# Summing the squares of twelve later norms on VectorE, and head norm pieces at half the rate

## The chip, the cores and the metric

The kernel runs on one core of one Trainium2 chip. The time is that of one execution on the device, in microseconds; several executions are taken and their median is given. One more execution is recorded by the hardware profiler, and everything called a row or a profile comes from that one.

## The reference

Two layers of a diffusion backbone run over 1024 latent tokens and 128 context tokens, 1024 channels each. What matters here is what stands at the start and the end of each half layer, and the norm of the attention heads:

```python
def rmsnorm(x, g):
    xf = x.astype(jnp.float32)
    y = xf * lax.rsqrt(jnp.mean(xf * xf, axis=-1, keepdims=True) + EPS)
    return y.astype(x.dtype) * g

def diff_head_out(o, subln_g, lam_init):
    o = rmsnorm(o, subln_g) * (1.0 - lam_init)        # per head, 128 channels

hc = modulate(rmsnorm(ctx, norm_g[i, 1]), m_ctx[3], m_ctx[4])
ctx = ctx + m_ctx[5] * sq_relu_mlp(hc, ff_w1[i], ff_w2[i])
...
y_prompt = rmsnorm(ctx, final_norm_g)
```

Layer 0 mixes its tokens by differential attention beside a state-space scan, layer 1 by a pooling mixer; each is followed by an MLP with 4096 hidden channels and a squared ReLU.

## The kernel before

The 1152 tokens lie in three blocks `b` of 384 (`BN`); block 2 holds 256 latent and 128 context tokens. Channels lie on the partitions, so `x[b]` is eight tiles (`k`) of 128 channels by 384 tokens, and a norm must add over the eight tiles and over the 128 partitions of each. The big products split each fp32 operand into a high and a low part (`blk`, `wh`/`wl`, `ph`/`pl`, all fp32r) and multiply three pairs of parts, so that TensorE's plain work comes in triples of 384-column products.

The norms that the change touches are the later ones: before the first MLP (norm 1), before the pooling mixer (norm 2), before the second MLP (norm 3) and at the end, each for three blocks, twelve in all. `norm_sums` is called with `done=False` for them. For each `k` ScalarE squares `x[b][k]` into a small tile (`r`, two of them; `ph` and `pl` for the final norms of blocks 1 and 2), and TensorE multiplies the square by a 128x32 tile of ones, on one of four column strips of the array (`tile_position`), into `nps`. So the sums of tiles `k` and `k + 4` stand on strip `k`. ScalarE copies `nps` to `s4`, and one product with `selbc`, in which only rows 0, 32, 64 and 96 hold 1/1024, adds the four strips and spreads the mean over all partitions (`npb`). `norm_root` then takes its -1/2 power in two ScalarE and four VectorE steps into `y`. The norms of the very first stage take `done=True`: their squares are made ahead, and they stay as they are.

The high and low parts of a block (`gains`: ScalarE writes `h_`, VectorE `l_`) don't need `y`, since `y` is multiplied in behind the first product of the MLP (`r<-p,y`). In a chunk of the MLP VectorE makes `r`, `s` and `pl` for every hidden tile and adds each second product to `x` (`x<-p,modc,x`); in the first MLP it also takes column sums for the modulation of layer 1 (`mj`).

The order of the work: a planner orders the instructions of each engine at build time, by its own costs, and the engines then run their queues in that order, each waiting for what an instruction needs. Only where an engine is pinned does it keep the order in which the code is written. In the attention, TensorE alone is pinned (`PINA = "T"`).

The attention loop has one step per block of 128 queries: nine per head (eight latent, one context), four heads, 36 in all and four more to drain. In a step TensorE computes the scores of block `i` (`SP`), transposes those of three steps before (`tp`), and multiplies by the values. VectorE takes the maxima (`nm`) and combines the two maps (`e`), ScalarE takes exponentials. When the last block of a head is done, `head_norm` of that head is appended to `norms`. It is a generator with nine pieces: the set-up of the root on [128, 9] numbers (`vv`), two pieces with two Newton steps each, and for each of three groups of blocks one piece in which VectorE scales `of` and one in which TensorE transposes it, ScalarE copies it to `og` and a store to `cS` is issued. The loop asks for pieces at the end of every step. The last head's run behind the loop, where nothing is pinned.

All instructions are recorded through one helper, so that their line in the profile is L86; tiles tell them apart.

Of the kernel before, what the change touches and what calls it, by code (L numbers as in the profile page):

```python
# [8 lines left out]
F32 = mybir.dt.float32  # L9
F32R = mybir.dt.float32r  # L10
I32 = mybir.dt.int32
AF = mybir.ActivationFunctionType
ALU = mybir.AluOpType
# [4 lines left out]
D = 1024  # L18
KT = 8
# [3 lines left out]
BN = 384  # L23
# [49 lines left out]
def build(nc, tc, a, o, probe=None):  # L73
    pinned = set()

    class Engine:
# [5 lines left out]
        def __getattr__(self, op):  # L82
            f = getattr(self.e, op)

            def call(*args, **kw):
                ins = f(*args, **kw)  # L86
                if self.name in pinned:
# [5 lines left out]
    V, A, T, P, S_ = (Engine(n, e) for n, e in (("V", nc.vector), ("A", nc.scalar), ("T", nc.tensor),  # L93
                                                ("P", nc.gpsimd), ("S", nc.sync)))
# [25 lines left out]
    def tt(e, out, x, y, op):  # L120
        return e.tensor_tensor(out, x, y, op=op)
# [19 lines left out]
    selbc = K([128, 128], F32, "selbc")  # L141
# [35 lines left out]
    GB = [2]  # L177
# [8 lines left out]
    psn = Pool("psn", side="left", space=PSUM)  # L186
# [69 lines left out]
    last_bc = [None]  # L256
# [2 lines left out]

    def norm_sums(xb, sq, s4, done=False):  # L260

        ps = psn([128, BN], F32, "nps", bufs=GB[0], tag="g")
        for k in range(KT):
            if not done:
                A.activation(sq(k), xb[k], AF.Square)
            g = k % 4
            T.matmul(ps[32 * g:32 * g + 32], ones32, sq(k, True), start=k < 4, stop=k >= 4, tile_position=(0, 32 * g))
        A.activation(s4, ps, AF.Copy)
        pb = psn([128, BN], F32, "npb", bufs=GB[0], tag="g")
        last_bc[0] = T.matmul(pb, selbc, s4, start=True, stop=True)  # L270
        return pb

    def norm_root(pb, y, u):

        A.activation(y, pb, AF.Ln, bias=epsc)
        A.activation(y, y, AF.Exp, scale=-0.5)
        tt(V, u, y, y, ALU.mult)
        stt(V, u, pb, epsc, u, ALU.add, ALU.mult)
        V.tensor_scalar(u, u, -0.5, 1.5, op0=ALU.mult, op1=ALU.add)
        tt(V, y, y, u, ALU.mult)  # L280
        return y

    def sq_tile(more=False):
        last = []

        def sq(k, again=False):
            if not again:
                last[:] = [hid([128, BN], F32, ("ph", "pl")[k % 2]) if more else HP([128, BN], F32, "r", bufs=2)]
            return last[0]

        return sq

    def norm_stats(xb, more=False):
        pb = norm_sums(xb, sq_tile(more), HP([128, BN], F32, "s", bufs=2))
        return norm_root(pb, HP([128, BN], F32, "y", bufs=YB[0]), HP([128, BN], F32, "s", bufs=2))

# [76 lines left out]
    def sums(b):  # L373
        return norm_sums(xs[b], lambda k, again=False: sqs[b][:, k], scratch(), True)
# [273 lines left out]
    for gi, g0 in enumerate(range(0, G, 3)):  # L648
        n = min(3, G - g0)
        for ri in range(2):  # L650
            p = pin_([128, 3, UC], F32, "pin", bufs=2)
            for j in range(n):
                g = g0 + j
# [90 lines left out]
    psn = Pool("psn", side="left", space=PSUM)  # L744
# [273 lines left out]
    def scores(i, m):  # L1018

        h, qb = work[i]  # L1020
        Q, Kd, Kl, Vv, l1 = hd[h]
        q0 = 128 * qb
        if m == 0:
            cur[i] = (AT([128, 2], F32, "nm", bufs=2), AT([128, 1], F32, "ll", bufs=2), [])
        nm, ll, ee = cur[i]
        if qb < 8:
            cuts, n, k0 = ((0, 512), (512, 1024), (1024, KEYS)), KEYS, 0
        else:
            cuts, n, k0 = ((0, TX),), TX, KEYS
        for c0, c1 in cuts:  # L1030
            T.matmul(SP[m][:, c0:c1], Q[m][:, q0:q0 + 128], Kd[m][:, k0 + c0:k0 + c1], start=True, stop=False)
            T.matmul(SP[m][:, c0:c1], Q[m][:, q0:q0 + 128], Kl[m][:, k0 + c0:k0 + c1], start=False, stop=True)

    def top(i, m):
        n = KEYS if work[i][1] < 8 else TX
        V.tensor_reduce(cur[i][0][:, m:m + 1], SP[m][:, 0:n], AX.X, ALU.max, negate=True)

    def exps(i, m):
        nm, ll, ee = cur[i]
        n = KEYS if work[i][1] < 8 else TX  # L1040
        e = AT([128, KEYS], F32, f"e{m}", bufs=4 - 2 * m)
        sum_ = ll[:, 0:1] if m else hd[work[i][0]][4][:, work[i][1]:work[i][1] + 1]
        last_set[0] = A.activation(e[:, :n], SP[m][:, 0:n], AF.Exp, bias=nm[:, m:m + 1], accum_out=sum_)
        ee.append(e[:, :n])

    def ratio(i):

        h, qb = work[i]
        ll = cur[i][1]
        cf = AT([128, 1], F32, "cf", bufs=2)  # L1050
        V.reciprocal(cf, ll)
        V.tensor_scalar(cf, cf, hd[h][4][:, qb:qb + 1], lamn, op0=ALU.mult, op1=ALU.mult)
        cur[i] = (cf, cur[i][2])

    def combine(i):
        cf, ee = cur.pop(i)
        stt(V, ee[0], ee[1], cf, ee[0], ALU.mult, ALU.add)
        st[i] = ee[0]
# [3 lines left out]
    def turn(i, k0):  # L1062

        if k0 == 0:
            wt[i] = AT([128, 10, 128], F32, "wt", bufs=2)
        n = 4 if work[i][1] < 8 else 1 - k0 // 4
        if n == 0:
            return
        pt = pT([128, 4, 128], F32, "tp", bufs=2)
        for j in range(n):  # L1070
            T.transpose(pt[:, j], st[i][:, 128 * (k0 + j):128 * (k0 + j + 1)], ident)
        A.activation(wt[i][:, k0:k0 + n], pt[:, :n], AF.Copy)

    def values(t, i):

        po = pT([128, 4, 128], F32, "tp", bufs=2)
        two = t < nw and work[t][1] < 8
        if two:
            for j in range(2):
                T.transpose(po[:, j], st[t][:, 128 * (8 + j):128 * (9 + j)], ident)  # L1080
        if i >= 0:
            h, qb = work[i]
            Vv = hd[h][3]
            nk = 10 if qb < 8 else 1
            for k in range(nk):
                T.matmul(po[:, 2], wt[i][:, k], Vv[:, k if qb < 8 else 10], start=k == 0, stop=k == nk - 1)

        def copies():
            if two:
                A.activation(wt[t][:, 8:10], po[:, 0:2], AF.Copy)  # L1090
            if i >= 0:
                if h not in ofs:
                    ofs[h] = RP([128, 9, 128], F32, "of", tag=("cos", "sin")[h % 2]), AT([128, 4, 9], F32, "vv", bufs=2)
                A.activation(ofs[h][0][:, qb], po[:, 2], AF.Copy)

        def squares():
            if i >= 0:
                of, vv = ofs[h]
                V.scalar_tensor_tensor(RP([128, 128], F32, "sq", tag="sc1"), of[:, qb], 1.0, of[:, qb], op0=ALU.mult,
                                       op1=ALU.mult, accum_out=vv[:, 3, qb:qb + 1])  # L1100

        return copies, squares
# [81 lines left out]
    loads, norms, done = None, [], None  # L1184
# [7 lines left out]
    for i, t in enumerate(turns):  # L1192
        if i == 1:
            pinned.update(PINA)
        v, tv = (tv, t) if t >= 0 else (-1, tv)
        if i < nw:
            h, qb = work[i]
            scores(i, 0)
            top(i, 0)
        if done:  # L1200
            done[0]()
        if 1 <= i <= nw:
            ratio(i - 1)
        if done:
            done[1]()
        if 0 <= t < nw:
            turn(t, 0)
        if i < nw:
            scores(i, 1)
            top(i, 1)  # L1210
        if 0 <= t < nw:
            turn(t, 4)
        if i < nw:
            exps(i, 0)
        if SO and i >= 2:
            next(side, None)
        if 1 <= i <= nw:
            combine(i - 1)
        if i < nw:
            exps(i, 1)  # L1220
        if not SO and i >= 2:
            next(side, None)
        done = values(t, v) if t >= 0 else None
        for _ in range(2):
            if norms and next(norms[0], 0) == 0:
                norms.pop(0)
        if v >= 1 and work[v - 1][1] == 8:
            norms.append(head_norm(work[v - 1][0]))
        if i < nw:
            if qb == 3 and h + 1 < HEADS:  # L1230
                loads = load_head(h + 1)
            if loads:
                next(loads, None)
# [29 lines left out]
    XP = Pool("xp", side="left")  # L1263
    BB = Pool("blkB", side="left")
    HP = Pool("hid", side="right")
    psn = Pool("ps2", side="left", space=PSUM)
    GB[0] = 2
    YB[0] = 3
# [8 lines left out]
    p2 = lambda shape: psn(shape, F32, "p2", bufs=4)  # L1277
    hid = lambda shape, dt, nm: HP(shape, dt, nm, bufs=4)
    cb = HP([128, 2, D], F32, "cb")

# [12 lines left out]
    def mod_vec(layer, t):  # L1293
# [4 lines left out]
        for r in range(2):  # L1298
            V.scalar_tensor_tensor(HP([128, D], F32, "mj"), raw, 1.0, cb[:, r], op0=ALU.mult, op1=ALU.mult,
                                   accum_out=modc[layer][:, t, r:r + 1])  # L1300
# [426 lines left out]
```

## Time and profile before

| | us |
|---|---|
| median of 3 executions | 2579.72 |
| lowest, highest | 2579.07, 2583.84 |
| profiled execution | 2578.7 |
| its span, first to last instruction | 2576.9 |
| TensorE products busy | 2449.6 (95%) |
| VectorE busy | 1748.6 (68%) |
| ScalarE busy | 883.8 (34%) |
| GpSimd busy | 259.6 (10%) |

Busy time is an average over stages with different limits. PE is TensorE's products, PEld its weight loads, DVE is VectorE, ACT ScalarE, POOL GpSimd. A product of two plain fp32 operands leaves two records, one of fp32r operands one. Products are pipelined, so the length of a record is longer than the distance to the next one; the distance between starts tells what the queue spends.

### The profile page before, as it was taken

The numbers are of one execution on the slowest core, as the hardware profiler recorded it, in microseconds if no ns is written. First come the engines' busy times: TensorE is split into PE (matmuls) and PEld (weight loads), VectorE is DVE, ScalarE is ACT, GpSimd is POOL, SyncE is SP. The second block draws the span as 40 slices with busy tenths as digits, with TensorE's granted clock in tenths as the row PEclk, the third lists the DMA queues.
The fourth block names the chain that finished last, engine by engine and source line by source line (L and its number), as shares of the span: only waits on it lengthen the run. The fifth ranks groups of instructions, "written<-read, shape, count | busy, mean of one in ns | idle before, by whom it ended". The sixth has DMA issues, their size and how long they took to land.

```text
span 2576.9 us, 36670 instructions
## 1 busy us (share of the span) xinstructions
PE 2449.6 (95%) x14262; PEld 2295.9 (89%) x14262; DVE 1748.6 (68%) x3498; ACT 883.8 (34%) x1675; POOL 259.6 (10%) x274
## 2 busy tenths in 40 slices
PE   7987897887899999999999999999999999999998
PEld 3876696787897999999999999779999999999996
DVE  7389875888687776877777655676555656555554
ACT  4453365776515222222222222562222222222114
POOL 5455512100000000000000000020000000000002
PEclk8998999999999999999999999999999999999999
DMA  6334689331263222222222110011111111011102
GB/s 241 83 107 130 190 199 235 71 92 48 78 225 116 73 82 79 84 83 81 90 80 89 50 33 25 1 50 42 50 41 42 50 33 50 33 50 42 42 9 74
DMA packets 106493, 210.89 MB, mean 82 GB/s; under 512 B 10576, under 2 KB 67664, under 8 KB 105936
## 3 DMA queue, kind: packets, MB, share of 16 engines
q1 hardware_dynamic: 104080, 203.01, 26.4%
q10 hardware_dynamic: 2240, 5.54, 0.6%
q8 instruction: 113, 1.85, 0.3%
q14 instruction: 60, 0.49, 0.1%
HBM read 176.95 MB, written 31.56 MB: 81 GB/s over the span
## 4 chain that ended last, share of the span: by engine, by line
PE 72%; DVE 7%; issue 4%; ACT 3%; DMA 3%; POOL 0%; SPq 0%; DVEq 0%; ACTq 0%; POOLq 0%
PE p L86 65%; PE nps L86 2%; PE pmm L86 2%; PE tp L86 1%; DVE nm L86 1%; ACT e L86 1%; PE SP L86 1%; DMA raw<-in_w_dram 1%; DVE e L86 1%; DMA raw<-in_mod_v_dram 1%; PE py L86 1%; DVE sc L86 1%; DVE mj L86 1%; DVE x L86 0%; DVE wl L86 0%
## 5 line engine op out<-in xcount | busy, mean ns | idle before, releaser
L86 PE MATMUL p<-blk,wh 128*128 128x384 f32 (+1 forms) x3072 | 794.9, 339 | 0.3 <-DVE r L86 0.3
L86 DVE SCALAR_TENSOR_TENSOR x<-p,modc,x 128x384 f32<-128x384 f32 (+2 forms) x1056 | 513.2, 513 | 162.7 <-PE p L86 158.5
L86 PEld LDWEIGHTS p<-blk,wh 128*128 128x128 f32 x3072 | 559.1, 189 | 13.3 <-issue 11.9
L86 PE MATMUL p<-blk,wl 128*128 128x384 f32 (+1 forms) x1536 | 521.4, 339 | 0.0
L86 PE MATMUL p<-ph,w2h 128*128 128x384 f32 x1536 | 515.1, 335 | 1.6 <-DVE x L86 1.6
L86 PE MATMUL p<-ph,w2l 128*128 128x384 f32 x1536 | 514.3, 335 | 0.0
L86 PE MATMUL p<-pl,w2h 128*128 128x384 f32 x1536 | 513.7, 334 | 0.0
L86 ACT ACTIVATE r<-r,cf 128x384 f32<-128x384 f32 (+2 forms) x256 | 129.9, 531 | 684.9 <-DVE r L86 684.8
L86 PEld LDWEIGHTS p<-blk,wl 128*128 128x128 f32 x1536 | 288.8, 188 | 6.5 <-issue 6.3
L86 PEld LDWEIGHTS p<-ph,w2h 128*128 128x128 f32 x1536 | 288.3, 188 | 6.9 <-DVE x L86 3.5
L86 PEld LDWEIGHTS p<-ph,w2l 128*128 128x128 f32 x1536 | 288.3, 188 | 2.6 <-issue 2.5
L86 PEld LDWEIGHTS p<-pl,w2h 128*128 128x128 f32 x1536 | 288.3, 188 | 0.8 <-issue 0.6
L86 DVE TENSOR_TENSOR r<-p,y 128x384 f32<-128x384 f32 x192 | 106.2, 553 | 207.4 <-PE p L86 194.3
L86 ACT ACTIVATE wh<-raw 128x1024 fp32r<-128x1024 f32 x80 | 84.8, 1060 | 346.1 <-PE p L86 312.2
L86 DVE SCALAR_TENSOR_TENSOR mj<-raw,cb 128x1024 f32<-128x1024 f32 x128 | 156.0, 1219 | 14.0 <-DMA raw<-in_mod_v_dram 12.9
L86 ACT ACTIVATE w2h<-raw 128x1024 fp32r<-128x1024 f32 x74 | 77.3, 1057 | 223.3 <-PE p L86 159.0
L86 PE MATMUL pmm<-lo,wh 128*128 128x384 f32 (+1 forms) x384 | 137.8, 359 | 7.3 <-DVE lo L86 7.1
L86 PE MATMUL pmm<-hi,wh 128*128 128x384 f32 (+1 forms) x384 | 141.3, 369 | 0.8 <-ACT wh L86 0.8
L86 PE MATMUL pmm<-hi,wl 128*128 128x384 f32 (+1 forms) x384 | 137.0, 357 | 1.2 <-DVE wl L86 1.2
L86 DVE TENSOR_TENSOR s<-r 128x384 f32<-128x384 f32 x192 | 106.4, 554 | 39.3 <-ACT r L86 39.1
L86 POOL TENSOR_TENSOR pl<-pl,mx 128x256 f32<-128x256 f32 x18 | 14.9, 827 | 1070.0 <-ACT pl L86 1070.0
L86 DVE TENSOR_TENSOR wl<-raw,wh 128x1024 fp32r<-128x1024 f32 x76 | 98.8, 1300 | 23.1 <-ACT wh L86 22.7
(281 smaller groups left out, 3348.7 us busy)
## 6 DMA issues: line engine op xcount, KB each, us to landing
raw<-in_w_dram SPq DMA_DIRECT2D x128, 512.0 KB, 3.6
raw<-in_mod_v_dram SPq DMA_DIRECT2D x64, 512.0 KB, 3.6
raw<-in_mod_w_dram SPq DMA_DIRECT2D x25, 512.0 KB, 4.9
raw<-in_w_in_dram SPq DMA_DIRECT2D x16, 512.0 KB, 4.8
Kd<-kS SPq DMA_DIRECT2D x32, 176.0 KB, 5.1
qS<-zz SPq DMA_DIRECT2D x12, 384.0 KB, 2.7
Q<-qS SPq DMA_DIRECT2D x32, 144.0 KB, 5.2
x<-in_x_dram SPq DMA_DIRECT2D x3, 1536.0 KB, 7.7
```

The lines of the kernel that those rows point to most:

```text
L86: ins = f(*args, **kw)
```

## The change

`norm_sums` with `done=False` no longer multiplies the squares by ones. The square of the first tile goes straight to `s4`, and VectorE adds the squares of the other seven tiles to it, one by one. A single product with `selbc` sums over the partitions and spreads. For that `selbc` is filled with 1/1024 in all rows after the attention. `nps` and its copy are gone for these twelve norms. In the attention loop one piece of the head norms is asked for per step, not two.

```diff
--- before.py
+++ after.py
@@ -259,10 +259,16 @@
 
     def norm_sums(xb, sq, s4, done=False):
 
+        if not done:
+            A.activation(s4, xb[0], AF.Square)
+            for k in range(1, KT):
+                A.activation(sq(k), xb[k], AF.Square)
+                tt(V, s4, s4, sq(k, True), ALU.add)
+            pb = psn([128, BN], F32, "npb", bufs=GB[0], tag="g")
+            last_bc[0] = T.matmul(pb, selbc, s4, start=True, stop=True)
+            return pb
         ps = psn([128, BN], F32, "nps", bufs=GB[0], tag="g")
         for k in range(KT):
-            if not done:
-                A.activation(sq(k), xb[k], AF.Square)
             g = k % 4
             T.matmul(ps[32 * g:32 * g + 32], ones32, sq(k, True), start=k < 4, stop=k >= 4, tile_position=(0, 32 * g))
         A.activation(s4, ps, AF.Copy)
@@ -1221,9 +1227,8 @@
         if not SO and i >= 2:
             next(side, None)
         done = values(t, v) if t >= 0 else None
-        for _ in range(2):
-            if norms and next(norms[0], 0) == 0:
-                norms.pop(0)
+        if norms and next(norms[0], 0) == 0:
+            norms.pop(0)
         if v >= 1 and work[v - 1][1] == 8:
             norms.append(head_norm(work[v - 1][0]))
         if i < nw:
@@ -1263,6 +1268,7 @@
     XP = Pool("xp", side="left")
     BB = Pool("blkB", side="left")
     HP = Pool("hid", side="right")
+    V.memset(selbc, 1.0 / D)
     psn = Pool("ps2", side="left", space=PSUM)
     GB[0] = 2
     YB[0] = 3
```

## Rows read from the trace of the kernel before

**Rows 1.** The page's chain that ended last, by line: share of the span.

```profile
PE p L86 65%; PE nps L86 2%; PE pmm L86 2%; PE tp L86 1%; DVE nm L86 1%; ACT e L86 1%; PE SP L86 1%; DMA raw<-in_w_dram 1%; DVE e L86 1%; DMA raw<-in_mod_v_dram 1%; PE py L86 1%; DVE sc L86 1%; DVE mj L86 1%; DVE x L86 0%; DVE wl L86 0%
```

**Rows 2.** Windows: length, then busy us of PE, PEld, DVE, ACT, POOL; clock, DMA.

```profile
795.00:840.00 45.00, 44.42 (x200) 28.40 (x199) 31.27 (x67) 29.72 (x64) 0.00 (x0) 1.00 0.22 71
840.00:1606.00 766.00, 764.43 (x4363) 763.09 (x4362) 538.24 (x1032) 171.29 (x276) 0.00 (x0) 1.00 0.23 71
1606.70:1655.00 48.30, 48.30 (x246) 37.10 (x244) 34.13 (x76) 30.61 (x64) 0.00 (x0) 1.00 0.00 1
1655.00:1684.00 29.00, 27.20 (x200) 22.75 (x200) 15.08 (x45) 12.83 (x32) 7.71 (x11) 1.00 0.01 2
1684.00:1756.00 72.00, 69.62 (x405) 50.31 (x404) 50.62 (x142) 45.21 (x99) 16.03 (x20) 1.00 0.16 51
2514.00:2534.00 20.00, 20.00 (x99) 14.72 (x98) 6.42 (x12) 8.73 (x18) 0.00 (x0) 1.00 0.00 1
2546.00:2562.30 16.30, 16.30 (x84) 10.89 (x84) 8.25 (x22) 11.76 (x26) 3.21 (x4) 1.00 0.12 41
```

**Rows 3.** Groups of instructions, whole span: busy us, mean ns, idle before.

```profile
L86 DVE TENSOR_TENSOR s<-r 128x384 f32<-128x384 f32 x192 | 106.4, 554 | 39.3 <-ACT r L86 39.1
...
L86 PE MATMUL nps<-r,ones 128*32 128x384 f32 x160 | 51.8, 498 | 0.8 <-ACT r L86 0.8
...
L86 ACT ACTIVATE r<-x 128x384 f32<-128x384 f32 x80 | 39.4, 518 | 42.5 <-PE nps L86 35.7 <-DVE x L86 6.8
```

**Rows 4.** Timeline of PE in the first norm: start us, us, instruction.

```profile
797.88 0.34 PE L86 MATMUL p<-blk,w2l 128*128 128x384 f32 x1
...
798.41 0.33 PE L86 MATMUL p<-blk,w2l 128*128 128x384 f32 x1
798.68 0.84 PE L86 MATMUL nps<-r,ones 128*32 128x384 f32 x4
799.45 0.62 PE L86 MATMUL p<-blk,w2h 128*128 128x384 f32 x2
799.90 0.33 PE L86 MATMUL p<-blk,w2l 128*128 128x384 f32 x1
...
800.34 0.83 PE L86 MATMUL nps<-r,ones 128*32 128x384 f32 x2
801.10 0.44 PE L86 MATMUL p<-blk,w2h 128*128 128x384 f32 x1
```

**Rows 5.** Timeline of DVE, POOL and ACT at the end.

```profile
2560.55 2.03 DVE L86 SCALAR_TENSOR_TENSOR x<-p,modc,x 128x256 f32<-128x256 f32 x6
...
2566.78 1.14 DVE L86 TENSOR_TENSOR s<-y 128x384 f32<-128x384 f32 x1 [4.20 <-ACT y L86]
...
2560.77 8.01 POOL L86 TENSOR_TENSOR x<-x,y 128x384 f32<-128x384 f32 x8 [13.09 <-ACT ph L86]
...
2564.12 0.49 ACT L86 ACTIVATE s<-nps 128x384 f32<-128x384 f32 x1 [0.92 <-PE nps L86]
2565.62 0.58 ACT L86 ACTIVATE y<-npb,epsc 128x384 f32<-128x384 f32 x1 [1.00 <-PE npb L86]
```

**Rows 6.** Waits of PE in the attention (total, times, longest), and three in its timeline.

```profile
PE tp L86 <- DVE of L86: 21.3, 4, 8.1
...
536.32 0.88 PE L86 MATMUL tp<-ident,of 128*128 128x128 f32 x3 [5.19 <-DVE of L86]
...
597.32 0.88 PE L86 MATMUL tp<-ident,of 128*128 128x128 f32 x3 [8.13 <-DVE of L86]
...
659.77 0.88 PE L86 MATMUL tp<-ident,of 128*128 128x128 f32 x3 [7.64 <-DVE of L86]
```

**Rows 7.** Windows right behind the three waits, columns as in Rows 2.

```profile
536.30:545.00 8.70, 8.68 (x49) 8.53 (x50) 2.76 (x11) 3.70 (x10) 0.00 (x0) 0.66 0.33 105
597.30:604.00 6.70, 6.68 (x44) 6.56 (x45) 3.50 (x12) 3.50 (x10) 0.00 (x0) 0.78 0.42 137
659.70:665.00 5.30, 5.23 (x26) 5.26 (x27) 2.40 (x8) 2.68 (x7) 0.00 (x0) 0.50 0.59 229
```

## The prediction

> **What bounds the kernel now.** I read the chain of waits first: TensorE holds nearly all of it, 65% in the plain products `p` alone, and `PE nps`, the products that sum a norm's squares, stand in it with 2%, some 50 us [rows 1]. Next the busy times by stretch, cut where the later norms lie [rows 2]: 795 to 840 us (the three norms before the first MLP), 1606.7 to 1655 and 1655 to 1684 (the three before pooling), 1684 to 1756 (the three before the second MLP), 2514 to 2534 and 2546 to 2562.3 (the final norms). The reader is to see two things. TensorE is busy through each of them (44.4 of 45, 48.3 of 48.3, 27.2 of 29, 69.6 of 72, 20 of 20, 16.3 of 16.3 us), so an instruction that leaves its queue there shortens the run unless something else is late. VectorE, which gets the new work, is busy 31.3, 34.1, 15.1, 50.6, 6.4 and 8.3 us of the same stretches: there is room, but not in all of them. The span is 2576.9 us, the profiled execution took 2578.7, and the median of the three runs is 2579.72, 1.0 above it; I sum against 2578.7 and add 1.0.
>
> **Removed: eight products per norm.** The table of groups [rows 3] gives 51.8 us of TensorE for ten of the twelve norms (160 records; each fp32 product leaves two), but a busy time doesn't say what the queue loses, so I count in the timeline [rows 4]. A plain triple `wh, wh, wl` repeats every 0.53 us (797.88 to 798.41). With one group of `nps` between, the same step takes 1.49 us (798.41 to 799.90): 0.96 us lost per group, since the queue pauses before and after it. A group of four records costs what a group of two does (798.68 to 799.45 is 0.77, 800.34 to 801.10 is 0.76). So the price goes by groups. Of such groups I count, in the stretches before the tail, 17 (three norms), 12 (two), 5, 20 (three) and 6, together 60 in ten norms; 60 x 0.95 = 57 us.
>
> A rule speaks for a smaller price: the Trainium skill, "TensorE: Matmul & The Clock Gate", Packing small matmuls, has tiles on different columns of the array run at once, four for little more than one. The row of four records agrees. By the rule alone a norm is two packs of four products, 2 x 0.77, ten norms are worth 15 us, and the time would be 42 us later, 2567. The trace differs because the squares come one at a time through two tiles, and so the products stand in five to seven groups; the measured 57 decides.
>
> The product with `selbc` stays, as do the squares. The copy to `s4` (ScalarE, 0.49 us, [rows 5]) goes; ScalarE isn't the bound in these stretches.
>
> **Added: seven additions per norm on VectorE.** The nearest row is `s<-r`, the same shape, SBUF to SBUF: 0.554 us [rows 3]; in a chain with itself a little more, 0.6. 84 of them are 47 to 50 us of VectorE. They are free where it idles and cost where it would then be the later engine. By stretch, with TensorE's time shortened by the groups:
> - 795 to 840: 45 - 16.2 = 28.8 us for TensorE; VectorE 31.3 + 21 x 0.554 = 42.9. 14 us too much. Part of it can wait: the column sums `mj` aren't needed at once, and the MLP behind leaves VectorE 766 - 538 = 228 us idle [rows 2]. What can't wait are the splits `blk`, the roots and `r, s, pl` of the first block. I take a loss of 5 (bounds 0 and 14).
> - 1606.7 to 1655: 48.3 - 11.4 = 36.9 against 34.1 + 7.8 = 41.9. 5 over; it holds back results that TensorE's accumulators wait for. Loss 4.
> - 1655 to 1684: 24.2 against 19.0. No loss.
> - 1684 to 1756: 72 - 19 = 53 against 50.6 + 11.6 = 62.2. 9 over, some of it passed on to the second MLP. Loss 6.
> - 2514 to 2534: 14.3 against 10.3. No loss.
>
> **The wait that is added.** The one product with `selbc` now waits for VectorE's last addition, and TensorE keeps its queue's order: plain products behind it wait too, and with them VectorE's next results. The trace shows no such wait. It is nothing where the planner puts the product late enough, and at most the whole chain, 0.52 + 7 x 0.6, about 5 us, where it stands right behind the squares. I take 0.2 us per norm, 2 in all, since the wait that it replaces (for the copy `s`) is mostly hidden too. The tiles of the squares are freed by VectorE now instead of TensorE, and `s4` is held from the first square on; both belong to tags of two that the MLP shares, which is in the same bounds.
>
> Ten norms: 57 - 5 - 4 - 6 - 2 = 40 us, between 15 and 57.
>
> **The tail.** VectorE writes the last parts of `x` until 2562.6, the copy `s` starts at 2564.12 and the first step of the root at 2565.62 [rows 5]. With the change TensorE gets through the last blocks about 5 us earlier, but VectorE must fit 14 additions, 7.8 us, into the 16.3 us in which it has 8.3 of work [rows 2]: it ends about when it ended before, and the copy goes (0.5). The danger is GpSimd: while it multiplies (2560.77 on), `s<-y` takes 1.14 instead of 0.55 us, so seven additions in its company cost 4 more. I take 1 us gained, bounds -4 and +5. The Trainium skill, "SBUF — State Buffer", Who interferes with whom, says that a VectorE instruction with two SBUF inputs contends with a GpSimd one that reads SBUF; the row agrees. By that rule all of the last norm's additions would be slow and the tail 4 us longer.
>
> **Head norm pieces, one per block.** TensorE runs in written order in the attention. Its largest waits there are `tp` for `DVE of`, 21.3 us in four [rows 6]: three stand before a head's first head norm transposes, 5.19, 8.13 and 7.64 us at 536, 597 and 660. The scaled `of` comes late because the twenty small steps of the root are strung between long VectorE instructions, and with two pieces a block the transposes follow the first step by two blocks only. With one a block they follow by four; a block is about 5.9 us ((597.32 - 536.32 - 8.13) / 9 between the first head norm transposes of two heads, the second stall taken off), so the small steps get some 12 us more and the stall should go. What is late next is VectorE, which was busy through the stalls. But it starves behind them, being busy only 2.76 of 8.7, 3.50 of 6.7 and 2.40 of 5.3 us, and TensorE comes out of them partly at the lower of its two clocks (granted 0.66, 0.78 and 0.50, against 1.00 in the stretches of [rows 2]) [rows 7]. 20.7 - 8.7 = 12 us of VectorE's idle time bound what the first two can give back. Behind the third TensorE is full to the end of the stage, so nearly all 7.6 us come back. Of head 2 one piece (three transposes, a copy, a store) falls behind the loop, under 1 us. I take 14, bounds 0 and 24. Memory traffic and other queues are the same: the stores `cS` move one to five blocks later and are read after the stage.
>
> **Sum.** 40 + 1 + 14 = 55; 2578.7 - 55 + 1.0 = 2524.7, say 2525 us.
>
> **Rivals.**
> - The additions cost twice what I take off. In the norm windows VectorE is 28 us over; if all of it comes back as TensorE waits instead of 15, and each `npb` waits 1.5 us, the norms give 57 - 28 - 15 = 14, and with the heads 28: 2552. For it: three stretches in which VectorE becomes the longer engine. Against: `mj` and the weight splits ahead of need can move.
> - The head norms give nothing, because VectorE sets the pace of the attention and the small steps are as many as before: 2539. Against: the idle time behind the stalls.
> - Nothing is lost: 57 + 5 + 24 = 86, so 2494. For it: before, the norms' latency was no shorter (eight squares at 0.52 us, each waiting for its product).
> - Slower than before: TensorE reaches the product with `selbc` early and stands there for the chain at every norm, while the additions queue on VectorE behind splits and `mj`. Its place is `npb`, its price the wait; it wins from the point where a norm's wait and what VectorE holds back exceed (57 + 14) / 10 = 7.1 us. With a 5.3 us chain and the 28 us over, that is 8.1 a norm: 2590. Against: VectorE is idle for 13.7 us of the first stretch and 14.2 of the second, and the planner counts the additions when it places the product.
> - That the planner, with other costs, reorders the work so that nothing moves: no change.
>
> **How the numbers follow.** Forecast with its own range of 2508 to 2538: 0.60. Heads give nothing: 0.12 (it lies at that range's upper edge). Additions cost twice: 0.13. Nothing lost: 0.09. No change: 0.02. Slower: 0.04. A range of 2500 to 2553 leaves out most of the fourth, half of the third and the last two, under 0.2. 0.2%, about what a measurement here tells from no change, is 5 us: faster 0.94, same 0.02, slower 0.04.
>
> **What would show it.** No `nps` on TensorE after 100 us; plain triples at 0.53 us right up to `npb`; 84 additions `s<-s,r` (or `ph`, `pl`) of about 0.55 us; no wait of `tp` for `of` above 1 us before the last head; VectorE's idle time in 795 to 830 near zero. I am wrong if TensorE waits at `npb` by more than 2 us a norm, if `r<-p` or `x<-p` become what TensorE waits for at the start of an MLP, if the attention's length stays, or if the end from VectorE's last `x` to the first step of the root grows beyond 3 us.

## The result: half of the gain that was forecast

| | before | after |
|---|---|---|
| median, lowest to highest, us | 2579.73, 2579.07 to 2583.84 | 2552.59, 2551.55 to 2554.24 |
| profiled execution, its span | 2578.7, 2576.9 | 2552.8, 2551.0 |
| TensorE, VectorE busy | 2449.6, 1748.6 | 2399.8, 1792.0 |

The ratio is 0.9892 (95% 0.9875 to 0.9909): 27 us faster, where 55 were forecast. The time lies at the upper edge of the stated range, 2500 to 2553, and outside the forecast's own, 2508 to 2538. To see where it differs I cut both traces at the same four events: the load of the Ln/Exp table behind the attention, the first `cf` of the first MLP's second-last chunk (what norm 1 does is in by then), the first band product of pooling (`p<-mx,ph`), the first 128x386 product of the second MLP. Lengths in us:

| stretch | before | after | difference | forecast |
|---|---|---|---|---|
| start to table load (attention) | 705.1 | 688.9 | -16.2 | -14 |
| table load to `cf` (norm 1) | 830.3 | 831.0 | +0.7 | -11 |
| `cf` to pooling's first band product (most of norm 2) | 132.0 | 127.0 | -5.0 | -10 |
| to the second MLP (rest of norm 2, norm 3 blocks 0 and 1) | 67.0 | 66.0 | -1.0 | -8 |
| second MLP to the end (norm 3 block 2, final norms) | 842.5 | 838.1 | -4.4 | -13 |

The forecast's column is its own terms: groups removed less VectorE's overrun, and 1 us for the tail in the last row, without the 2 us for waits at `npb`. The groups are put where they lie in the trace before, 17, 15, 15 and 13 in the last four rows, at 0.95 us each. So the attention did a little better than forecast, and the norms with the tail gave 9.7 us instead of 41.

How far such differences can be trusted is seen where two kernels share their code behind the attention: the kernel before and the run with the new head norm pieces alone (below) agree within 0.4 us in each of the last four stretches, the changed kernel and the run with the new norms alone within 2.1 us.

The waits of TensorE say why: first those in the attention (480 to 700 us), then those from 760 us to the end, each with total, times and longest. They answer to [rows 6].

```profile
PE SP L86 <- ACT e L86: 13.8, 18, 2.2
PE tp L86 <- ACT of L86: 1.9, 1, 1.9
...
PE npb L86 <- DVE s L86: 37.4, 7, 10.3
PE p L86 <- DVE w2l L86: 4.3, 1, 4.3
PE p L86 <- DVE x L86: 3.7, 6, 0.9
```

`tp` no longer waits for VectorE's `of`: 21.3 us are gone, 1.9 for ScalarE have come, and the waits of `SP` for `e` have grown from 11.7 to 13.8 us. And `npb` waits 37.4 us for VectorE's sums; before it waited 1.2 us in all, for the copy. Here is one such place, the start of the first MLP, in the timeline: TensorE, then VectorE and ScalarE.

```profile
805.46 0.33 PE L86 MATMUL p<-blk,wl 128*128 128x386 f32 x1
810.69 1.27 PE L86 MATMUL npb<-s,selbc 128*128 128x384 f32 x2 [4.89 <-DVE s L86]
820.35 1.65 PE L86 MATMUL npb<-s,selbc 128*128 128x384 f32 x2 [8.39 <-DVE s L86]
...
822.44 0.52 PE L86 MATMUL p<-blk,wl 128*128 128x384 f32 x1
...
806.84 0.56 DVE L86 TENSOR_TENSOR s<-s,r 128x384 f32<-128x384 f32 x1
807.32 1.22 DVE L86 SCALAR_TENSOR_TENSOR mj<-raw,cb 128x1024 f32<-128x1024 f32 x1
...
808.46 0.56 DVE L86 TENSOR_TENSOR s<-s,r 128x384 f32<-128x384 f32 x1
808.93 1.22 DVE L86 SCALAR_TENSOR_TENSOR mj<-raw,cb 128x1024 f32<-128x1024 f32 x1
...
810.08 0.56 DVE L86 TENSOR_TENSOR s<-s,r 128x384 f32<-128x384 f32 x1
...
811.70 1.22 DVE L86 TENSOR_TENSOR wl<-raw,wh 128x1024 fp32r<-128x1024 f32 x1
...
817.29 1.22 DVE L86 TENSOR_TENSOR w2l<-raw,w2h 128x1024 fp32r<-128x1024 f32 x1
818.42 1.88 DVE L86 TENSOR_TENSOR s<-s,r 128x384 f32<-128x384 f32 x3
820.22 1.01 DVE L86 TENSOR_TENSOR r<-p,y 128x384 f32<-128x384 f32 x2
...
809.05 0.52 ACT L86 ACTIVATE r<-x 128x384 f32<-128x384 f32 x1 [1.09 <-DVE s L86]
```

An addition takes 0.56 us as forecast, but the next one starts 1.62 us later (806.84, 808.46, 810.08). Two things are seen in between: a column sum `mj` of 1.22 us on VectorE, and a square on ScalarE that could only start when the addition had freed one of the two `r` tiles. That square is done at 809.57, while `mj` keeps VectorE until 810.08, so here it is `mj` that sets the pace. Where nothing stands between, three additions take 1.88 us (818.42). The second and longer wait, 8.39 us, has no `mj` in it: there the root of block 1 and two weight splits of 1.22 us (`wl`, `w2l`) stand beside the additions. TensorE has computed block 0's two hidden tiles by 805.8, and the two products `npb` (blocks 1 and 2) stand next in its queue. What would empty the accumulators, `r<-p,y`, writes the same two `r` tiles and comes only at 820.22, behind the last addition.

The waits cost more than their length. These are windows of the stretch before the second MLP (columns as in [rows 2]):

```profile
1663.00:1712.93 49.93, 40.59 (x268) 37.38 (x267) 43.13 (x118) 31.77 (x70) 16.40 (x18) 0.79 0.16 52
1672.00:1674.00 2.00, 0.00 (x0) 0.00 (x0) 2.00 (x7) 2.00 (x5) 0.00 (x0) 1.00 0.00 0
1676.00:1678.00 2.00, 1.91 (x4) 0.74 (x4) 2.00 (x5) 0.57 (x2) 0.00 (x0) 0.50 0.00 0
1682.00:1684.00 2.00, 2.00 (x11) 2.00 (x11) 0.76 (x3) 0.00 (x0) 0.09 (x1) 0.50 0.00 0
1688.00:1690.00 2.00, 2.00 (x20) 2.00 (x19) 1.12 (x4) 0.00 (x0) 0.00 (x0) 1.00 1.00 397
```

TensorE stands from 1671.8 to 1675.75 for `npb`; behind that its granted clock is 0.50, the lower of its two levels (1.2 GHz), until about 1685. In 2 us it gets through 11 products at that clock and 20 at 1.00. Before, the clock was 1.00 all through ([rows 2], fourth and fifth line). VectorE is at 2.00 of 2.00 while TensorE stands, and 43.1 us busy of 49.9 in the whole window.

Not every loss shows as a wait for `npb`. In the stretch before pooling there is none; there TensorE waits the 4.3 us for `w2l`, and 3.3 us in five shorter waits, four of them for VectorE.

The end, first VectorE's last `x` and its additions, then TensorE, ScalarE and GpSimd; it answers to [rows 5].

```profile
2530.00 0.34 DVE L86 SCALAR_TENSOR_TENSOR x<-p,modc,x 128x128 f32<-128x128 f32 x1
2530.26 0.55 DVE L86 TENSOR_TENSOR s<-s,pl 128x384 f32<-128x384 f32 x1
2530.84 1.23 DVE L86 TENSOR_TENSOR s<-s,ph 128x384 f32<-128x384 f32 x1
...
2537.24 1.16 DVE L86 TENSOR_TENSOR s<-s,pl 128x384 f32<-128x384 f32 x1
...
2538.46 1.65 PE L86 MATMUL npb<-s,selbc 128*128 128x384 f32 x2 [10.29 <-DVE s L86]
...
2540.20 0.58 ACT L86 ACTIVATE y<-npb,epsc 128x384 f32<-128x384 f32 x1 [9.22 <-POOL x L86]
...
2530.22 9.99 POOL L86 TENSOR_TENSOR x<-x,y 128x384 f32<-128x384 f32 x8 [12.77 <-ACT ph L86]
```

From the last `x` (2530.34) to the first step of the root 9.9 us pass, against 3.0 before (2562.58 to 2565.62). All seven additions come behind the last `x`; VectorE did block 1's root and `x` first. Six of them take 1.16 to 1.23 us beside GpSimd's products, instead of 0.55. The Trainium skill, "SBUF — State Buffer", Who interferes with whom, says that a VectorE instruction with two SBUF inputs contends with a GpSimd one that reads SBUF. Those six rows agree.

### The profile page after: what moved, and what is told of

The parts are those of the page before. It is cut to its first block, busy times and chain, and to the rows that moved or that the text cites. A ratio compares the mean times of both kernels' runs of the same rounds, so it can differ in the third digit from the quotient of the medians.

```text
span 2551.0 us, 36404 instructions
## 1 busy us (share of the span) xinstructions
PE 2399.8 (94%) x14070; PEld 2296.1 (90%) x14070; DVE 1792.0 (70%) x3583; ACT 877.2 (34%) x1663; POOL 267.0 (10%) x274
## 4 chain that ended last, share of the span: by engine, by line
PE 64%; DVE 11%; issue 5%; ACT 4%; DMA 4%; POOL 1%; SPq 0%; POOLq 0%; DVEq 0%; ACTq 0%
PE p L86 61%; DVE mj L86 2%; DVE blk L86 1%; DMA raw<-in_w_dram 1%; DVE sc L86 1%; DMA raw<-in_mod_v_dram 1%; PE SP L86 1%; DVE nm L86 1%; ACT e L86 1%; PE tp L86 1%; DVE x L86 1%; DVE s L86 1%; ACT blk L86 1%; DVE zz L86 1%; DVE w2l L86 1%
## 5 line engine op out<-in xcount | busy, mean ns | idle before, releaser
L86 DVE SCALAR_TENSOR_TENSOR mj<-raw,cb 128x1024 f32<-128x1024 f32 x128 | 156.1, 1220 | 13.6 <-DMA raw<-in_mod_v_dram 12.6
```

## Experiments

Every ratio is against the kernel before on the same chip; the changed kernel stands at 0.9892.

**The two parts alone.**

```diff
 # heads only: kernel before, with
-        for _ in range(2):
-            if norms and next(norms[0], 0) == 0:
-                norms.pop(0)
+        if norms and next(norms[0], 0) == 0:
+            norms.pop(0)
 # norms only: changed kernel, with these lines as before
```

> The head norm pieces one per block alone, the later norms as before. The trace of the changed kernel reaches the table load at the attention's end 16.2 us earlier (688.88 against 705.10), so if the two parts don't touch each other: 2579.7 - 16.2 = 2563.5 us. Rival: the gain of the attention is there only because what follows it is shorter too (loads that the norms' buffers free earlier); then 2570 or more.

Measured: 2560.07, ratio 0.9927 (0.9910 to 0.9943), 18.0 us.

> The later norms changed, the head norm pieces two per block as before. If the parts are independent, 2552.6 + 16.2 = 2568.8 us, a gain of 11 where 41 was forecast. Rival: the norms lose because they come earlier against the loads behind the attention; then alone they gain more, 2560 or less.

Measured: 2569.01, ratio 0.9964 (0.9951 to 0.9977), 9.1 us. 18.0 + 9.1 is the 27.1 of both; with intervals of 3 to 4 us to either side the sum shows that the parts are independent within that, not to the last digit. The norms are where the forecast's gain is missing.

**Wait or work?** Two theories: TensorE loses by standing at `npb` (and by the clock behind it), or VectorE is simply the longer engine and `npb` is where it shows.

```diff
 # e3: the same additions, but npb doesn't wait for them (not in the final norms)
-                tt(V, s4, s4, sq(k, True), ALU.add)
+                d = s4 if key[0] == 4 else sq(k, True)
+                tt(V, d, s4, sq(k, True), ALU.add)
...
 # e4: TensorE has something to do while it would stand
+            for _ in range(5 if key in ((1, 1), (1, 2), (3, 0), (3, 1), (3, 2)) else 0):
+                T.matmul(pb, selbc, xb[7], start=True, stop=True)
             last_bc[0] = T.matmul(pb, selbc, s4, start=True, stop=True)
...
```

> As the changed kernel, but in the nine middle norms (before the first MLP, before pooling, before the second MLP) each of the seven additions adds the first square to its own square tile, so VectorE does the same number of additions of the same shape, and the product with selbc takes the first square alone. Seven eighths of the sum are left out there; the final norms are untouched. Wait theory (what the change loses is TensorE standing at npb behind a drawn-out chain of additions, and the lower clock that follows): the 27.2 us of waits at npb in these norms go, and some 14 us of half speed behind them (20 us of the stretch before the second MLP and 8 of the first MLP at 0.50, worth half): about 2511 us. VectorE theory (VectorE is the longer engine there, and npb only the place where it shows): TensorE then waits for r<-p,y, blk or x instead, and at most 8 us come back: 2545 to 2553.

Measured: 2538.62, ratio 0.9843 (0.9828 to 0.9858), between the two. The stretches tell more: from the table load to `cf` 821.3 instead of 831.0, but from pooling to the end 59.2 + 843.9 = 903.1 instead of 66.0 + 838.1 = 904.1. Ahead of the first MLP the wait theory holds, 10 us come back. Ahead of the second MLP the VectorE theory holds: the wait has moved to the weight splits, as TensorE's waits from 1631 to 1740 us show.

```profile
PE p L86 <- DVE wl L86: 9.6, 1, 9.6
PE p L86 <- DVE ph L86: 3.2, 2, 1.9
```

> As the changed kernel, but ahead of the product with selbc in five norms (blocks 1 and 2 before the first MLP, all three before the second MLP) five needless products of the same shape are put into the same accumulator; they need only the block's last x, and are overwritten. They fill some 3.3 us of each wait (0.65 a product at full clock). If TensorE's standing is what takes its clock from 1.00 to 0.50 behind the waits, the half-speed time of 1676 to 1685, 1700 to 1709, 1726 to 1729 and 820 to 825 shrinks to a third and about 8 us come back: 2544. If the clock falls for another reason, the products only lengthen the queue where the wait is shorter than they are: 2552 to 2557.

Measured: 2548.97, ratio 0.9881 (0.9867 to 0.9896); its interval holds the changed kernel's 0.9892, so the whole time shows little. The window from pooling's first band product to the second MLP shows the clock:

```profile
1642.46:1700.62 58.16, 56.31 (x419) 50.74 (x417) 47.10 (x139) 36.43 (x82) 22.13 (x27) 1.00 0.11 37
```

58.2 us instead of 66.0, at a clock of 1.00 instead of 0.84, although ten needless products (6.6 us) are in it: without the standing the clock doesn't fall, and TensorE's own work of that stretch takes 56.3 - 6.6 = 49.7 us instead of 56.7. But from the second MLP to the end it takes 4.5 us longer (842.6). It holds the last five needless products (3.3 us), and TensorE waits there for `wl` and still for `npb`, as its waits from 1590 to 1740 us show:

```profile
PE p L86 <- DVE wl L86: 3.1, 1, 3.1
PE npb L86 <- DVE s L86: 2.5, 1, 2.5
```

VectorE is late all the same. Ahead of the first MLP the ten products ran together before the standing began, and changed nothing (830.5).

**What draws the chain out.**

```diff
 # e5: column sums one chunk later
-        if c < 12:
+        if 0 < c < 13:
...
-                mod_vec(1, 4 * c + t)
-            if c == 11 and b == 2:
+                mod_vec(1, 4 * c - 4 + t)
+            if c == 12 and b == 2:
 # e8: eight square tiles instead of two
-                last[:] = [hid([128, BN], F32, ("ph", "pl")[k % 2]) if more else HP([128, BN], F32, "r", bufs=2)]
+                last[:] = [hid([128, BN], F32, ("ph", "pl")[k % 2]) if True else HP([128, BN], F32, "r", bufs=2)]
 # e7: the very last norm by strips and copy (the copy scaled, since selbc is full)
-        if not done:
+        if not done and key != (4, 2):
             A.activation(s4, xb[0], AF.Square)
...
+            if not done:
+                A.activation(sq(k), xb[k], AF.Square)
...
-        A.activation(s4, ps, AF.Copy)
+        A.activation(s4, ps, AF.Copy, scale=1.0 if done else 1.0 / 32)
```

> As the changed kernel, but the column sums mj of the first MLP begin one chunk later (chunks 1 to 12 instead of 0 to 11), so VectorE has none of them beside the norms before that MLP. In the changed kernel four of them (1.14 us each) stand between the additions there, 805 to 812 us. If the wait at npb there (4.89 and 8.39 us) is VectorE's overrun, about 4.6 us and the half-speed time behind it come back: from the attention's end to the second chunk 831 us would become 825, in all 6 less than the changed kernel: 0.9869 of before (2546.5 against 2579.7). If the chain would be drawn out anyway (two square tiles, an addition waiting for a square and a square for an addition), VectorE puts something else between or stands idle: 2550 to 2553, ratio 0.989.

Measured: 2544.82, ratio 0.9862 (0.9845 to 0.9880). Table load to `cf` takes 823.8, 7.2 less, as expected; the two longest waits there are 2.29 and 6.95 us instead of 4.89 and 8.39.

> As the changed kernel, but all later norms take their square tiles from ph and pl (four of each) instead of the two r tiles, so that ScalarE can square ahead and VectorE can add in a run. If the hand-over of two tiles between ScalarE and VectorE is what draws the chain out (each addition 1.6 us after the one before where 0.47 is possible), the 27.2 us of waits at npb fall to below 12 and the half-speed time behind them to below half: 20 us or more come back, ratio to before 0.981 (2532 against 2579.7). If VectorE's amount of work sets the pace, the additions only move: 2548 to 2555, ratio 0.988 to 0.990.

Measured: 2545.73, ratio 0.9866 (0.9845 to 0.9887), neither figure. The waits at `npb` fall from 37.4 to 23.6 us, and table load to `cf` takes 823.9. The additions don't follow each other faster there: with `mj` between, they still stand 1.61 us apart. But the squares no longer hold `r`, so `r<-p,y` comes among the additions, at 802.53 instead of 820.22, and TensorE has other work until its `npb` at 807.17, before which it doesn't wait:

```profile
802.53 0.55 DVE L86 TENSOR_TENSOR r<-p,y 128x384 f32<-128x384 f32 x1
...
804.52 0.55 DVE L86 TENSOR_TENSOR s<-s,ph 128x384 f32<-128x384 f32 x1
...
806.13 0.55 DVE L86 TENSOR_TENSOR s<-s,pl 128x384 f32<-128x384 f32 x1
```

Before the second MLP nothing is won (65.4), and new waits stand beside the old ones, here from 700 us to the end:

```profile
PE npb L86 <- DVE s L86: 23.6, 9, 10.3
PE p L86 <- DVE w2l L86: 3.4, 1, 3.4
PE p L86 <- DVE pl L86: 3.3, 1, 3.3
PE p L86 <- DVE r L86: 3.0, 1, 3.0
PE p L86 <- DVE ph L86: 2.7, 2, 1.9
```

> As the changed kernel, but the very last norm (final, block 2) sums by the eight strip products and the copy, as before. In the changed kernel 9.9 us pass from VectorE's last x to the first step of the last root, in which seven additions run beside GpSimd at 1.16 to 1.23 us instead of 0.55; in the kernel before it was 3.1. If those additions in GpSimd's company are the tail's loss, 5 to 7 us come back: ratio to before 0.9868 (2545.6 to 2547.6 against 2579.7). If the tail is bound by GpSimd's products of block 1 or the stores anyway: 2551 to 2553, ratio 0.989.

Measured: 2546.54, ratio 0.9868 (0.9848 to 0.9889), as expected if the additions beside GpSimd are the tail's loss. From the second MLP to the end 832.9 us instead of 838.1; from the last `x` (2532.13) to the root 3.1:

```profile
2531.78 0.35 DVE L86 SCALAR_TENSOR_TENSOR x<-p,modc,x 128x128 f32<-128x128 f32 x1
...
2535.22 0.58 ACT L86 ACTIVATE y<-npb,epsc 128x384 f32<-128x384 f32 x1 [1.06 <-PE npb L86]
```

> The additions on VectorE kept, with three changes together that gave 6 to 8 us each alone: column sums one chunk later, eight square tiles instead of two, and the very last norm by strip products. By stage, the first two shorten the same stretch (from the attention's end to the second chunk 831.0 to 823.8 us in either), the third only the tail (838.1 to 832.9 from the second MLP on). If the first two take away the same wait, the sum is 7 + 1 + 5 = 13 to 14 us: ratio 0.984. If they take away different parts of it (work in the way, and the hand-over of the tiles), 20 us: ratio 0.9815. Neither reaches the fp32r products (0.9756) if VectorE's amount of work is the rest.

Measured: 2537.68, ratio 0.9830 (0.9812 to 0.9847), by the ratios 16 us less than the changed kernel. Table load to `cf` takes 820.8: of the 7 us of each remedy 10 remain together, so they take away mostly the same wait. Pooling to the second MLP stays at 66.1: there none of it helps.

**The strips without VectorE.** If VectorE's part is the loss, sums that need neither strips nor VectorE should give the forecast's 40 us.

```diff
-            A.activation(s4, xb[0], AF.Square)
-            for k in range(1, KT):
+            pb = psn([128, BN], F32, "npb", bufs=GB[0], tag="g")
+            for k in range(KT):
                 A.activation(sq(k), xb[k], AF.Square)
-                tt(V, s4, s4, sq(k, True), ALU.add)
-            pb = psn([128, BN], F32, "npb", bufs=GB[0], tag="g")
-            last_bc[0] = T.matmul(pb, selbc, s4, start=True, stop=True)
+                last_bc[0] = T.matmul(pb, selr[0], sq(k, True), start=k == 0, stop=k == KT - 1)
...
 # e6: square tiles of type fp32r, selr[0] = selbc read as fp32r; e9: both fp32
```

> As the changed kernel, but VectorE adds nothing: ScalarE writes each square rounded to fp32r, and eight accumulating fp32r products with the full 128x128 selbc sum and spread it; no strips, no copy, one product per square at 0.17 us like a plain one. The 60 groups at 0.95 us of before stay removed (57 us), and 12 x 8 products at 0.17 us come in their place (16 us). If what the change lost is VectorE's additions and the waits they bring (both theories), the norms give 41 us and the tail 0 to 2: with the attention's 16 to 18, ratio to before 0.977 (2520 against 2579.7). If a group of products pauses TensorE whatever its mode (0.5 us or more a group, 60 groups), about 2537, ratio 0.9835.

Measured: 2517.43, ratio 0.9756 (0.9739 to 0.9774), 63 us faster than the kernel before and 35 faster than the changed one: the fastest of this study. It isn't the same arithmetic: the squares are of type fp32r, of which the big products take two parts for each fp32 operand. A plain triple with two of its products in between takes 1.13 us from 779.99 to 781.12 instead of 0.53, so one loses 0.30 us here, where a group of strip products lost 0.96 [rows 4]:

```profile
779.99 0.34 PE L86 MATMUL p<-blk,w2l 128*128 128x384 f32 x1
780.25 0.44 PE L86 MATMUL npb<-r,selbc 128*128 128x384 f32 x1
780.52 0.34 PE L86 MATMUL p<-blk,w2h 128*128 128x384 f32 x1
780.70 0.40 PE L86 MATMUL npb<-r,selbc 128*128 128x384 f32 x1
780.94 0.34 PE L86 MATMUL p<-blk,w2h 128*128 128x384 f32 x1
781.12 0.34 PE L86 MATMUL p<-blk,w2l 128*128 128x384 f32 x1
```

By stretch, against before: -10.8, -8.7, -14.2 and -8.1 us behind the table load, 41.8 in all. Two windows, pooling to the second MLP and the first part of the second MLP, show TensorE's clock near 1.00. `npb` is no longer late there, but VectorE still is at the second MLP's start, where TensorE waits 5.25 us for `r` (last row):

```profile
1628.57:1681.39 52.82, 51.44 (x409) 49.20 (x408) 42.49 (x129) 37.69 (x85) 20.38 (x27) 1.00 0.16 51
1681.39:1736.95 55.56, 50.31 (x271) 49.19 (x270) 36.42 (x73) 18.75 (x39) 0.00 (x0) 0.94 0.18 58
...
1697.29 1.01 PE L86 MATMUL p<-blk,wh 128*128 128x384 f32 x2 [5.25 <-DVE r L86]
```

> As the kernel with eight fp32r products per norm, but the squares stay fp32: eight accumulating fp32 products with the full 128x128 selbc, nothing on VectorE, no strips, no copy. In the trace with filler products ten such products in a row take 6.61 us, 0.66 each, against 0.17 in fp32r. If TensorE's own time for the products is all that counts, ten norms cost 10 x 8 x 0.66 = 53 us where the 60 groups cost 57, and with the attention's 17 the time is about 2558 against 2579.7, ratio 0.9915. If each group of fp32 products also pauses TensorE between fp32r products (0.2 to 0.3 us, as 0.96 lost for a group of 0.77 in the kernel before), 12 to 18 us more: 2573, ratio 0.997. If the gain of the fp32r kernel comes from VectorE being free and not from the type, this one is as fast: 2520, ratio 0.977.

Measured: 2546.72, ratio 0.9869 (0.9852 to 0.9885): 11 us better than the nearest expectation. That one left out that the separate product with `selbc` goes as well, 10 x 0.66 us; with it 57 + 7 - 53 = 11, and the stretches behind the table load give 12.6. There is no pause between fp32 and fp32r products (below). So even in fp32, eight whole products a norm on TensorE do no worse than one product and seven additions on VectorE: 12.6 us behind the table load against 9.7, or 11.2 in the trace with the new norms alone. That they do better is not shown, neither by these figures nor by the whole times. TensorE doesn't wait for `npb` in this kernel.

## Why the prediction was half right

- **Attention, forecast 14: right.** The three waits of `tp` for `of` went, as reasoned, and 16.2 us came back in the trace, 18.0 in the run of that part alone. The figure has its scatter: the table load comes between 683.8 and 690.7 us in the ten traces with the new pieces, at 705.1 and 706.2 in the two with the old. One bound was misread: the 12 us for the first two waits hold VectorE's idle time behind all three; behind the first two it is 9.1 us.
- **Groups removed, forecast 57: borne out.** With it, and 7 for the separate product, the fp32 kernel's 12.6 come out as 11, and the fp32r kernel's 41.8 lie within 40 to 50 (its 80 products at 0.30 to 0.17 us).
- **What was lost of them.** Of the 57 us 9.7 came. With the groups at 0.95 us in each stretch, 17 were lost ahead of the first MLP, 9 in the stretch before pooling, 15 from pooling to VectorE's last `x`, and 6 from there to the end. The forecast had 5, 4 and 6, 2 for waits at `npb`, and 1 gained in the tail.
- **Waits at `npb`, forecast 2: wrong, and the step that failed.** They are 37.4 us, 10.3 of them at the end. The prediction took 0.2 us a norm since the planner would place the product late enough, and bounded a wait by a chain of 0.6 us a link, 5 us. The planner placed it too early in seven of twelve norms. The 0.6 a link holds only where nothing stands between the additions; with `mj` between a link takes 1.6 us, and with a root and weight splits between one wait is 8.39. Taking `mj` away or giving the squares other tiles gave 7 us each and 10 together ahead of the first MLP, where even the fp32r kernel is only 1.3 us shorter (819.5).
- **VectorE's overrun, forecast 15: too low.** From pooling to the end 21 us were forecast and 5.4 came. Not awaiting the sum, filling the wait or giving the squares other tiles give next to nothing there: 903.1, 900.8 (with 9.9 us of needless products in it) and 903.3 against 904.1, and the three remedies 901.0, although the tail alone became 5 us shorter. Taking the additions off VectorE gives 887.2, of which 7.4 are the tail's (13.2 instead of 20.6 us from the last `x` to the end). That VectorE was 9 us over before the second MLP stood in the prediction; that a late VectorE makes TensorE stand, and that its clock then halves for some 9 us more, did not, although [rows 7] had shown the same behind the waits of the attention.
- **The tail, forecast 1 with -4 as its lower bound: wrong.** The end from the last `x` to the root grew from 3.0 to 9.9 us, the sign that was named for being wrong, and to the end of the run from 14.3 to 20.6. The danger had its price (4 us); that all seven additions would come behind the last `x` was not seen.
- **The range held by luck.** Its upper edge, 2553, is 0.4 us above the median, less than the executions differ among themselves. The rival "the additions cost twice", with 2552, has the measured time and names what happened, VectorE's work coming back as waits of TensorE. But its terms are off and largely cancel: it took 15 us for waits at `npb` where 37.4 were measured, 14 from the norms where 9.7 came, and 14 from the attention where 16 to 18 came.

What stays open: how the loss before the second MLP divides between the 0.56 us of the additions as such and their order on VectorE among `x`, `blk` and weight splits. No run changed that order alone, and since the planner orders each kernel anew, an edit to the norms can move other work too.

## What to carry to other kernels

Work that leaves a full engine is worth its queue time only if what replaces it isn't awaited in order by that engine: price the chain link by link, with what stands between the links on the other queue, and ask which other work waits for the tiles that it holds. Count a standing TensorE with the time it then spends at its lower clock. And before moving a sum to another engine, try it in the type and tile shape of the work around it: if the type is allowed, eight products of a norm, whole and in fp32r, lost 0.30 us each or less where they were counted, where a strip group lost 0.96.

## What was not expected of the hardware

In these traces, products of fp32 and of fp32r that both use the whole array follow each other without a pause. Ten fp32 products in a row took 6.61 us, 0.66 each; in the kernel with eight fp32 products two of them (four records) and a plain one pass in 1.46 us, from 802.43 to 803.89, and 2 x 0.66 + 0.17 is 1.49:

```profile
802.43 1.45 PE L86 MATMUL npb<-r,selbc 128*128 128x384 f32 x4
803.42 0.63 PE L86 MATMUL p<-blk,wl 128*128 128x386 f32 x1
803.89 0.34 PE L86 MATMUL p<-blk,wh 128*128 128x386 f32 x1
```

So of the 0.96 us that a strip group cost [rows 4], 0.66 can be put down to the time of one fp32 product, and by difference, an estimate, the other 0.3 came with the strips. The pause that the prediction saw around each group is not one for the type.
